# Small steps around the choice of the first expert's tokens, moved or shortened, and three index products put elsewhere

## The chip, the cores and the metric

The program runs on one core of a Trainium2 chip. The metric is the device time of one execution in microseconds (us); the time before is the median of three runs. The engines are PE (matrix products; PEld loads its weights), DVE (vector), ACT (scalar and activation), POOL (GpSimd) and SP, which here only issues DMAs. All engines run side by side, each takes its own instructions in order, and they meet through semaphores.

## What is computed

One layer of an encoder: a mixing sub-layer (half Fourier, half windowed attention), then a mixture of experts in which every expert picks its own tokens. The change touches the second sub-layer and the last tile of the first.

```python
D_MODEL, SEQ, N_EXPERTS, D_EXPERT, CAPACITY_FACTOR = 1024, 1024, 16, 1024, 2

def expert_choice_moe(h, w_router, w_gate, w_up, w_down):
    B, S, D = h.shape
    cap = CAPACITY_FACTOR * S // N_EXPERTS           # 128 tokens per expert
    aff = jax.nn.softmax(jnp.einsum('bsd,de->bse', h, w_router).astype(jnp.float32), axis=-1)
    g, idx = lax.top_k(aff.transpose(0, 2, 1), cap)
    xin = jax.vmap(lambda hb, ib: hb[ib])(h, idx)
    a = jnp.einsum('becd,edf->becf', xin, w_gate)
    u = jnp.einsum('becd,edf->becf', xin, w_up)
    y = jnp.einsum('becf,efd->becd', jax.nn.silu(a) * u, w_down)
    y = y * g[..., None].astype(y.dtype)
    return jax.vmap(lambda yb, ib: jnp.zeros((S, D), yb.dtype)
                    .at[ib.reshape(-1)].add(yb.reshape(-1, D)))(y, idx)

# in the layer:
x = x + g1 * mixed
h2 = rmsnorm(x, norm_ffn_g[l]) * (1.0 + sc2) + sh2
x = x + g2 * expert_choice_moe(h2, w_router[l], w_gate[l], w_up[l], w_down[l])
```

All arrays are float32.

## The kernel before

The 1024 tokens are eight tiles of 128. The mixing sub-layer goes over the tiles; `oproj(t)` is the output projection of a tile, after which `x2` (the residual stream) and `h2` (its normed and modulated copy) of the tile are known. `last_tile` does this for tile 7 in smaller steps: `x2` is flipped on PE and multiplied by the router's weights (L822, L832), POOL raises the mean square to the power -0.5 (`rs`, L837), and `affinity` makes the softmax `aff` of the tile (L883 to L893). The rest of `last_tile` makes `h2`: a product with `G2_r` on DVE (L838), a scaling by `rs` on ACT in two halves (L842, L850), an addition of `sh2_r` on POOL in two halves (L852), and then SP writes `h2` to the DRAM tensor `h2d` (L1271). Between these stand four 32-wide transposes that turn the ranked scores of the older tiles, `R`, into `bestw` (L844, L847).

`choose(e)` then finds, for one expert, the position that each token gets among its 128 chosen (`pos`), by counting on PE and DVE. It is called for expert 0 and, after expert 0's tokens are fetched, for expert 1. `gather_a(e)` (L1306) compares `pos` with the numbers 1 to 128 (`slots`) and makes a one-hot matrix `oneh`, eight compares of a 128x128 tile, on DVE for experts 0 to 3 and on POOL for the others. `gather(e)` multiplies the eight tiles of `oneh` with the token numbers and gates on PE (L1313, the index products), adds two columns to the index (L1317), and POOL fetches the 128 rows of `h2d` by an indirect DMA into the only buffer `xe` (L1319). `busy` issues bf16 products of no use that keep PE running (L1168).

Then come the experts. An expert is 12 products of 2 k-blocks each: four for `w_gate` (`ga`), four for `w_up` (`up`), four for `w_down`, the last four of expert e during expert e+1 (`put`). They are counted by `step[0]`: P0 to P3 are `ga` of expert 0, P4 to P7 its `up`, P8 to P11 `ga` of expert 1, P12 to P15 `put(0)`, P16 to P19 `up` of expert 1, P20 to P23 `ga` of expert 2, and so on. P0 to P5 are done in plain float32 from the loaded weights (L1292). The others use a split: ACT copies a unit of weights to a float32r part `wh` (L86), DVE subtracts to get the rest `wl` (L87), and PE does three products (L81 to L83). A split for a later product is issued as far ahead as four buffers of `wh` and `wl` allow. The gathered rows `xe` and the hidden values `hs` are flipped by `flip` (L1339, eight transposes into two PSUM banks named `pt`, of which there are only two in all) and split in the same way into `t0h`, `t0l`, `t1h`, `t1l`.

What belongs to the choice for experts 1 to 3 is the generator `selection`. `product` draws a number of steps from it ahead of each product (`rest`), so a `yield` in it is a place between two products. `thresholds` sorts the last two tiles' scores and finds the positions for the other 15 experts: a 16-wide diagonal `dg`, a product with it (L1259), the compares `gq` and the counting (L1174, L1176).

The order of the work is fixed at the end of the kernel: PE, DVE and POOL keep the written order from `mark[0]` (the start of `last_tile`) on, SP from the write of `h2d` on, ACT from `selection` on; before that a scheduler may place ACT's work. `tc.issue_after(i)` queues what is written in its block behind instruction `i` where both are on one engine; it makes no engine wait for another.

## Time and profile before

| | us |
|---|---|
| median of 3 runs | 981.7 (980.85 to 984.77) |
| the profiled execution | 983.92 |
| its span, first to last instruction | 982.1 |
| PE busy / DVE busy / ACT busy / POOL busy | 937.9 / 787.6 / 629.2 / 411.5 |

The profile's times are from the span's start. A row of the timeline gives start, duration, engine, line, operation, what it writes and reads, and in brackets how long the engine sat idle before it and whose event ended that. Several instructions of one kind in a row are one line (x8), whose duration runs from the first start to the last end. Plain float32 products stand as two instructions each. PEclk is the TensorE clock that was granted, 1.00 for 2.4 GHz and 0.50 for 1.2 GHz.

### The profile page before, as it was taken

How to read it: one execution, taken by the hardware profiler on the slowest of the kernel's cores; microseconds unless marked ns; L12 is line 12 of the kernel's file. 1: busy time of each engine (PE TensorE's matmuls, PEld its weight loads, DVE VectorE, ACT ScalarE, POOL GpSimd, SP SyncE). 2: the span in 40 equal slices, each digit the busy share in tenths (PEclk: the TensorE clock that was granted, in tenths of full speed). 3: DMA queues.
4: the chain of work that ended last, by engine and by line, in shares of the span. 5: the costliest groups of instructions: out<-in, count | busy, mean ns of one | idle time of the engine just before them, and what ended most of it. 6: DMA issues, size and time to landing. Idle time of an engine off the chain costs nothing.

```text
span 982.1 us, 13289 instructions
## 1 busy us (share of the span) xinstructions
PE 937.9 (95%) x4788; PEld 736.2 (75%) x4788; DVE 787.6 (80%) x1231; ACT 629.2 (64%) x839; POOL 411.5 (42%) x247
## 2 busy tenths in 40 slices
PE   4999999989999999899899999999999999999996
PEld 2678777657777776468788888888888888888885
DVE  1436787788777968988888988998898898889894
ACT  2464533657566653247578777777777777877771
POOL 1007455100000002203449767876976876792201
PEclk9999999989999999999999999999999999999998
DMA  8977556462222248699999999999999999999912
GB/s 283 345 259 269 183 207 223 135 191 81 80 76 93 76 177 317 255 408 408 357 358 409 383 387 404 393 385 385 411 387 388 408 384 388 389 407 384 386 65 44
DMA packets 91787, 283.98 MB, mean 289 GB/s; under 512 B 8156, under 2 KB 25744, under 8 KB 91592
## 3 DMA queue, kind: packets, MB, share of 16 engines
q1 hardware_dynamic: 86856, 266.32, 70.9%
q0 software_dynamic: 4864, 16.80, 6.7%
q8 instruction: 38, 0.62, 0.3%
q14 instruction: 29, 0.24, 0.1%
HBM read 263.79 MB, written 21.40 MB: 290 GB/s over the span
## 4 chain that ended last, share of the span: by engine, by line
PE 82%; DVE 9%; ACT 3%; DMA 2%; issue 1%; SPq 1%; POOLq 0%; POOL 0%; ACTq 0%; DVEq 0%
PE pa L81 17%; PE pa L83 17%; PE pa L82 17%; PE pu L376 6%; PE pt L1339 3%; PE pj L81 2%; PE yp L728 2%; PE pj L82 2%; PE pj L83 2%; DVE ws L123 2%; PE pt L715 2%; PE pa L1292 2%; PE lg L686 1%; DMA raw<-in_w_ada_dram 1%; PE pv L376 1%
## 5 line engine op out<-in xcount | busy, mean ns | idle before, releaser
L87 DVE TENSOR_TENSOR wl<-raw,wh 128x2048 fp32r<-128x2048 f32 (+1 forms) x189 | 422.6, 2267 | 53.9 <-ACT wh L86 52.9
L86 ACT ACTIVATE wh<-raw 128x2048 fp32r<-128x2048 f32 (+1 forms) x189 | 355.4, 1896 | 79.5 <-PE pa L82 62.6
L1306 POOL TENSOR_SCALAR oneh<-tri_f,pos 128x128 bf16<-128x128 f32 x96 | 212.5, 2228 | 15.1 <-PE pt L1313 14.7
L81 PE MATMUL pa<-wh,t1h 128*128 128x512 f32 x384 | 151.4, 394 | 0.0
L83 PE MATMUL pa<-wl,t1h 128*128 128x512 f32 x384 | 149.6, 390 | 0.0
L82 PE MATMUL pa<-wh,t1l 128*128 128x512 f32 x384 | 149.5, 389 | 0.0
L81 PE MATMUL pa<-wh,t0h 128*128 128x512 f32 x360 | 143.2, 398 | 0.0
L82 PE MATMUL pa<-wh,t0l 128*128 128x512 f32 x360 | 140.9, 391 | 0.0
L83 PE MATMUL pa<-wl,t0h 128*128 128x512 f32 x360 | 140.9, 391 | 0.0
L83 PEld LDWEIGHTS pa<-wl,t1h 128*128 128x128 f32 x384 | 72.1, 188 | 15.1
L82 PEld LDWEIGHTS pa<-wh,t1l 128*128 128x128 f32 x384 | 72.1, 188 | 14.3
L81 PEld LDWEIGHTS pa<-wh,t1h 128*128 128x128 f32 x384 | 72.1, 188 | 14.3
L83 PEld LDWEIGHTS pa<-wl,t0h 128*128 128x128 f32 x360 | 68.0, 189 | 14.3
L82 PEld LDWEIGHTS pa<-wh,t0l 128*128 128x128 f32 x360 | 68.0, 189 | 13.7 <-issue 0.2
L81 PEld LDWEIGHTS pa<-wh,t0h 128*128 128x128 f32 x360 | 68.0, 189 | 13.7 <-issue 0.2
L1319 POOL DMA_INDIRECT xe<-h2d,idx x16 | 18.4, 1147 | 136.4 <-DVE gt L1329 122.6
L809 POOL TENSOR_TENSOR rs<-ss,mhalf 128x1 f32<-128x1 f32 x7 | 3.9, 558 | 170.8 <-DVE ss L807 146.8
L1357 POOL DMA_INDIRECT out_dram<-ys,idx x15 | 49.3, 3287 | 45.9 <-DVE ys L1356 41.8
L1354 POOL TENSOR_TENSOR ys<-ys,g_r 128x512 f32<-128x512 f32 x28 | 50.0, 1804 | 43.1 <-ACT ys L1353 43.1
L278 ACT ACTIVATE hf<-pt,sh1c,G1c 128x128 f32<-128x128 f32 (+1 forms) x56 | 22.6, 482 | 35.6 <-PE pt L271 35.6
L376 PE MATMUL pu<-wh,hh 128*128 128x512 f32 x128 | 42.6, 417 | 1.0 <-ACT hh L86 0.9
L689 DVE CUSTOM_DVE_ANT_0 sb<-lg,bias,sink 128x384 f32<-128x384 f32 (+1 forms) x64 | 35.2, 579 | 9.9 <-PE lg L687 4.9
(344 smaller groups left out, 1644.2 us busy)
## 6 DMA issues: line engine op xcount, KB each, us to landing
raw<-in_w_gate_dram SPq DMA_DIRECT2D x64, 1024.0 KB, 9.1
raw<-in_w_up_dram SPq DMA_DIRECT2D x64, 1024.0 KB, 8.9
raw<-in_w_down_dram SPq DMA_DIRECT2D x63, 1024.0 KB, 8.8
raw<-in_w_ada_dram SPq DMA_DIRECT2D x16, 1024.0 KB, 7.6
raw<-in_w_ada_dram SPq DMA_DIRECT2D x16, 512.0 KB, 9.6
xt<-in_x_dram SPq DMA_DIRECT2D x8, 512.0 KB
raw<-in_w_out_dram SPq DMA_DIRECT2D x4, 1024.0 KB, 4.9
raw<-in_x_dram SPq DMA_DIRECT2D x8, 512.0 KB
```

What stands on the lines that cost most here:

```text
L81: PE.matmul(o, lh, rh, start=start, stop=False)
L82: PE.matmul(o, ll, rh, start=False, stop=False)
L83: return PE.matmul(o, lh, rl, start=False, stop=stop)
L86: ACT.activation(hi, src, AF.Copy)
L87: return (eng or DVE).tensor_tensor(lo, src, hi.bitcast(F32), op=OP.subtract)
L278: ACT.activation(hf[:, a * w:a * w + w], tp[:, a * w:a * w + w], AF.Identity, scale=G1c[:, kc:kc + 1], bias=sh1c[:, kc:kc + 1])
L376: PE.matmul(acc[:, :c1 - c0], lhs, r[kc][:, c0:c1], start=first, stop=(kc == 7 and r is w_l), skip_group_check=c0 == 1024)
L689: DVE.tensor_tensor_reduce(sb[:, :wid], lg[:, :wid], bias[:, kv * 4 + i, j0:j0 + wid], 1.0, sk[:, i:i + 1], op0=OP.add, op1=OP.max, accum_ ...
L1306: (POOL if t < shared else DVE).tensor_scalar(oneh[:, t, :], slots, pos[:, t, e:e + 1], None, op0=OP.is_equal)
L1339: PE.transpose(p[:, k * 128:k * 128 + 128], src[:, (4 * b + k) * 128:(4 * b + k + 1) * 128], ident)
L1354: POOL.tensor_tensor(ys[:, cs_], ys[:, cs_], g2_r[:, cs_], op=OP.mult)
L1357: POOL.indirect_dma_start(out=out2, out_offset=bass.IndirectOffsetOnAxis(ap=idx[:, :1], axis=0), in_=ys, in_offset=None, compute_op=OP.add)
```

## The change

In `last_tile`, PE gets two filling products of 128 columns ahead of the first pair of flips and one ahead of the second; the product with `G2_r` moves from ahead of `affinity` into `aside`, which stands between the maximum and the exponential; the four transposes of `R` all stand behind `affinity`; the copy `bestT` stands ahead of it; and POOL's two additions of `sh2_r` are written in a block `issue_after(after["aff"].ins)`. The numbers 1 to 128 are copied to bf16 (`slots_b`), and `gather_a` compares with that copy. In the experts, `xf` (the flipped rows of expert 0) is made in three parts, and the third, with the gate product of expert 0, moves behind P0; `selection` is drawn 0 steps ahead of P0, 1 ahead of P1, 5 up to P9 and 3 from then on; the index products of expert 1 move from behind P0 to behind P1, those of expert 2 from behind P12 to behind P11, and those of expert 3 from behind P21 to behind P15.

The order of DVE around the softmax of tile 7 before (`ss` is the mean square, `lg` the router's logits, `raw<-raw,G_r` the product with `G2_r`, `best` is `bestw`, `acc` the first count of `choose(0)`):

```order
L835 TENSOR_TENSOR ss<-ss 128x1
L838 TENSOR_TENSOR raw<-raw,G_r 128x512
L883 SCALAR_TENSOR_TENSOR lg<-pj,rs,cb 128x16
L885 TENSOR_REDUCE mx<-lg 128x1
L844 STREAM_TRANSPOSE best<-R 32x32 x3
L892 RECIPROCAL rsm<-sm 128x1
L893 TENSOR_SCALAR aff<-ex,rsm 128x16
L847 STREAM_TRANSPOSE best<-R 32x32
```

And now:

```order
L837 TENSOR_TENSOR ss<-ss 128x1
L885 SCALAR_TENSOR_TENSOR lg<-pj,rs,cb 128x16
L887 TENSOR_REDUCE mx<-lg 128x1
L844 TENSOR_TENSOR raw<-raw,G_r 128x512
L894 RECIPROCAL rsm<-sm 128x1
L895 TENSOR_SCALAR aff<-ex,rsm 128x16
L849 STREAM_TRANSPOSE best<-R 32x32 x4
```

The product with `G2_r` has changed places with three of the transposes. POOL's rows at this place are the same before and now, and the second addition waits for ACT alone in both; these are the rows now, with the semaphores that each waits for in brackets (DMAHW are DMA queues):

```order
L839 TENSOR_TENSOR rs<-ss,mhalf 128x1 [waits DVE_49,Pool_49]
L846 COPY bestT<-R 16x128
L854 TENSOR_TENSOR raw<-raw,sh_r 128x512 [waits DMAHW1_49,DMAHW0_49,DMAHW3_49,PE_49,Activation_49]
L854 TENSOR_TENSOR raw<-raw,sh_r 128x512 [waits Activation_49]
L1323 DMA xe<-h2d,idx 128x1024 [waits DMAHW3_49,DMAHW2_49,DMAHW4_49,DMASW0_49,DVE_49]
```

Neither addition waits for DVE, where `aff` is made. On ACT, whose order is not fixed here, the first half of the split of P6's weights now stands between the exponential and the second scaling of `h2`.

PE from the fetched rows of expert 0 to the index products of expert 1 before (`ys` is the storage of `xf`; L1384 is the gate product of expert 0, each of its eight and of the eight of L1313 with a weight load ahead):

```order
L1377 MATMUL pt<-ident,xe 128x128 x8
L1384 LDWEIGHTS oneh
L1384 MATMUL pt<-aux,oneh 128x4
...
L1292 MATMUL pa<-raw,ys 128x512 x4
L1313 LDWEIGHTS oneh
L1313 MATMUL pt<-aux,oneh 128x6
...
L937 MATMUL pt<-ident,aff 32x128
```

And now:

```order
L1382 MATMUL pt<-ident,xe 128x128 x4
L1296 MATMUL pa<-raw,ys 128x512 x4
L1382 MATMUL pt<-ident,xe 128x128 x4
L1394 LDWEIGHTS oneh
L1394 MATMUL pt<-aux,oneh 128x4
...
L1296 MATMUL pa<-raw,ys 128x512 x4
L1317 LDWEIGHTS oneh
L1317 MATMUL pt<-aux,oneh 128x6
```

Four plain products (P0) now stand ahead of the last four flips, and four more (P1) ahead of the index products of expert 1.

DVE from the diagonal `dg` to the one-hot matrix of expert 3 before (`cn` and `pos` come from the counting; `wl` is a split of one unit of weights):

```order
L1256 TENSOR_SCALAR dg<-ident,R 16x16
...
L1306 TENSOR_SCALAR oneh<-tri_f,pos 128x128 x8
L87 TENSOR_TENSOR wl<-raw,wh 128x2048 x3
...
L87 TENSOR_TENSOR wl<-raw,wh 128x2048 x6
L87 TENSOR_TENSOR t0l<-pt,t0h 128x512 x2
L87 TENSOR_TENSOR wl<-raw,wh 128x2048
L1424 TENSOR_TENSOR hs<-hs,pa 128x512 x2
L1306 TENSOR_SCALAR oneh<-tri_f,pos 128x128 x8
L87 TENSOR_TENSOR wl<-raw,wh 128x2048 x2
L87 TENSOR_TENSOR t1l<-pt,t1h 128x512 x2
```

And now:

```order
L1260 TENSOR_SCALAR dg<-ident,R 16x16
...
L87 TENSOR_TENSOR t0l<-pt,t0h 128x512 x2
L87 TENSOR_TENSOR wl<-raw,wh 128x2048
L1183 SCALAR_TENSOR_TENSOR cn_4683<-pa,gq_4611 128x240
L1268 TENSOR_TENSOR pos<-cn_4683 128x8x15
L1310 TENSOR_SCALAR oneh<-slots_b,pos 128x128 x8
L87 TENSOR_TENSOR wl<-raw,wh 128x2048
...
L87 TENSOR_TENSOR wl<-raw,wh 128x2048 x3
L1310 TENSOR_SCALAR oneh<-slots_b,pos 128x128 x8
```

The one-hot matrix of expert 3 has moved from behind the product `hs` of expert 1 (ahead of the two splits and the flip's rest `t1l`) to a place four splits behind that of expert 2; ahead of the latter stands one split more.

The diff:

```diff
--- before.py
+++ after.py
@@ -825,6 +825,8 @@
             DVE.tensor_tensor(h2[:, c], o[:, 256 * q:256 * q + 256], g1_r[:, c], op=OP.mult)
             DVE.tensor_tensor(x2[:, c], x2[:, c], h2[:, c], op=OP.add)
             f = pt()
+            for _ in range(2 - q):
+                PE.matmul(f[:, 256:384], ident, ident, start=True, stop=True)
             for k in range(2):
                 PE.transpose(f[:, k * 128:k * 128 + 128], x2[:, c.start + k * 128:c.start + k * 128 + 128], ident)
             ACT.activation(x2T[:, 4 + 2 * q:6 + 2 * q].rearrange("p a b -> p (a b)"), f[:, :256], AF.Copy)
@@ -835,21 +837,21 @@
         after["ss"] = DVE.tensor_tensor(ss[:, 0:1], ss[:, 0:1], ss[:, 1:2], op=OP.add)
         rs = p3.tile([128, 1], F32, name="rs", bufs=2)
         POOL.tensor_tensor(rs, ss[:, 0:1], mhalf[:, 0:1], op=OP.pow)
-        DVE.tensor_tensor(h2[:, 512:], x2[:, 512:], G2_r[:, 512:], op=OP.mult)
         R, = ranked
 
         def aside():
             ACT.activation(h2[:, :512], h2[:, :512], AF.Copy, scale=rs)
-            for b in range(3):
-                DVE.transpose(bestw[32 * b:32 * b + 32, :], R[:, 32 * b:32 * b + 32])
-
+            DVE.tensor_tensor(h2[:, 512:], x2[:, 512:], G2_r[:, 512:], op=OP.mult)
+
+        POOL.tensor_copy(bestT, R[:16])
         affinity(t, p, rs, aside)
-        DVE.transpose(bestw[96:, :], R[:, 96:])
-        POOL.tensor_copy(bestT, R[:16])
+        for b in range(4):
+            DVE.transpose(bestw[32 * b:32 * b + 32, :], R[:, 32 * b:32 * b + 32])
         with tc.issue_after(after["exp"].ins):
             ACT.activation(h2[:, 512:], h2[:, 512:], AF.Copy, scale=rs)
-        for c in (slice(0, 512), slice(512, D)):
-            POOL.tensor_tensor(h2[:, c], h2[:, c], sh2_r[:, c], op=OP.add)
+        with tc.issue_after(after["aff"].ins):
+            for c in (slice(0, 512), slice(512, D)):
+                POOL.tensor_tensor(h2[:, c], h2[:, c], sh2_r[:, c], op=OP.add)
         lastx.append((rows, x2, h2))
 
     def x2_flip(t, b, x2):
@@ -1135,7 +1137,9 @@
     aside = [POOL.tensor_copy(tri, r1_f)]
     tri_f = rt.tile([128, 3, 128], F32, name="tri_f")
     SP.dma_start(tri_f, t_in["k_tri"][1:4].rearrange("a p c -> p a c"))
-    slots, both = tri_f[:, 0, :], tri_f[:, 1:3, :].rearrange("p a c -> p (a c)")
+    slots_b = rt.tile([128, 128], BF, name="slots_b")
+    aside.append(POOL.tensor_copy(slots_b, tri_f[:, 0, :]))
+    both = tri_f[:, 1:3, :].rearrange("p a c -> p (a c)")
     below = tri_f[:, 2, :]
     ones_b = rt.tile([128, 128], BF, name="ones_b")
     aside.append(POOL.memset(ones_b, 1.0))
@@ -1283,7 +1287,7 @@
     def product(acc, xh, xl, la=3, halves=False):
         n = step[0]
         u = n % 4
-        drain(itertools.islice(rest, 5 if n < 9 else 3))
+        drain(itertools.islice(rest, 0 if n == 0 else 1 if n == 1 else 5 if n < 10 else 3))
         ahead(min(la, 1 + n // 2))
         step[0] += 1
         if n in PLAIN:
@@ -1303,7 +1307,7 @@
         shared = 0 if e < 4 else NT
         oneh = wk.tile([128, NT, 128], BF, name="oneh", bufs=1)
         for t in range(NT):
-            (POOL if t < shared else DVE).tensor_scalar(oneh[:, t, :], slots, pos[:, t, e:e + 1], None, op0=OP.is_equal)
+            (POOL if t < shared else DVE).tensor_scalar(oneh[:, t, :], slots_b, pos[:, t, e:e + 1], None, op0=OP.is_equal)
         return oneh
 
     def gather(e, oneh):
@@ -1371,30 +1375,35 @@
         cut_unit(2)
         cut_unit(2)
     xf = wk.tile([128, D], F32, name="ys", bufs=1).rearrange("p (k c) -> p k c", c=128)
-    for k0, n in ((0, 2), (2, 2), (4, 4)):
+
+    def xf_flip(k0, n):
         p = pt()
         for k in range(n):
             PE.transpose(p[:, k * 128:k * 128 + 128], gs[0][2][:, (k0 + k) * 128:(k0 + k + 1) * 128], ident)
         ACT.activation(xf[:, k0:k0 + n], p[:, :n * 128].rearrange("p (a b) -> p a b", b=128), AF.Copy)
+
+    xf_flip(0, 2)
+    xf_flip(2, 2)
     xh, xl = (wk.tile([128, 8, 128], F32R, name=f"t0{x}", bufs=1) for x in "hl")
 
+
     def selection():
+        xf_flip(4, 4)
         p = pt()
         for t in range(NT):
             PE.matmul(p[:, :4], oneh0[:, t, :], aux[:, t, 0, 2:], start=(t == 0), stop=(t == NT - 1))
         gates(0, p[:, :4])
-        yield from wait(4)
         split(xh, xl, xf)
         oneh = gather_a(1)
-        yield from wait(3)
+        yield
         gather(1, oneh)
         for _ in thresholds():
             yield
         for e in (2, 3):
-            while step[0] < 12 * e - 16:
+            while step[0] < 7 * e - 6:
                 yield
             o = gather_a(e)
-            yield from wait(7)
+            yield from wait(9 - 2 * e)
             gather(e, o)
 
     rest = selection()
```

## Rows read from the trace of the kernel before

**Rows 1.** The page's first part, busy time of each engine over the span.

```profile
PE 937.9 (95%) x4788; PEld 736.2 (75%) x4788; DVE 787.6 (80%) x1231; ACT 629.2 (64%) x839; POOL 411.5 (42%) x247
```

**Rows 2.** What PE waited for from 380 us to the end: who, for whom, us in total, times, longest.

```profile
PE pt L1313 <- DVE t1l L87: 3.6, 1, 3.6
PE pt L1313 <- DVE oneh L1306: 1.3, 2, 1.0
```

**Rows 3.** One stretch of the expert loop: its length, PE's busy time and instructions, granted clock, busy share of the DMA engines, GB/s.

```profile
540.00:575.00 35.00, 35.00 (x171) 1.00 1.03 390
```

**Rows 4.** Timeline around the softmax of tile 7.

```profile
387.76 0.68 DVE L838 TENSOR_TENSOR raw<-raw,G_r 128x512 f32<-128x512 f32 x1
387.99 0.87 POOL L837 TENSOR_TENSOR rs<-ss,mhalf 128x1 f32<-128x1 f32 x1 [2.15 <-DVE ss L835]
...
388.90 0.72 ACT L842 ACTIVATE raw<-raw,rs 128x512 f32<-128x512 f32 x1 [1.01 <-POOL rs L837]
...
389.26 0.62 DVE L844 STREAM_TRANSPOSE best<-R 32x32 f32<-32x32 f32 x3
...
389.70 2.50 POOL L852 TENSOR_TENSOR raw<-raw,sh_r 128x512 f32<-128x512 f32 x2 [0.60 <-ACT raw L842]
...
390.14 0.86 DVE L893 TENSOR_SCALAR aff<-ex,rsm 128x16 f32<-128x16 f32 x1
...
391.90 0.48 DVE L1205 SCALAR_TENSOR_TENSOR junk<-pt,best,ones 128x256 bf16<-128x256 f32 x1 [0.66 <-PE pt L1195]
```

**Rows 5.** The same two kinds of instruction in all tiles: shortest, median and longest in ns, first and last start in us.

```profile
L809 POOL TENSOR_TENSOR rs<-ss,mhalf x7: 548/548/599, 245.2 to 374.4; 128x1 f32<-128x1 f32 x7
...
L893 DVE TENSOR_SCALAR aff<-ex,rsm x8: 217/232/861, 253.1 to 390.1; 128x16 f32<-128x16 f32 x8
```

**Rows 6.** PE in single microseconds around the same place, columns as in the group of the expert loop.

```profile
385.00:386.00 1.00, 0.35 (x4) 1.00 1.02 410
...
389.00:390.00 1.00, 1.00 (x5) 0.50 1.03 410
```

**Rows 7.** Compares and scalings on DVE: total and mean of one (us, ns) for two widths of one scaling, and the eight compares of expert 0 in the timeline.

```profile
L704 DVE TENSOR_SCALAR sb<-sb,rin 128x384 f32<-128x384 f32 x48 | 16.9, 416 | 0.2
...
L704 DVE TENSOR_SCALAR sb<-sb,rin 128x256 f32<-128x256 f32 x16 | 4.6, 349 | 0.1
...
395.60 1.65 DVE L1306 TENSOR_SCALAR oneh<-tri_f,pos 128x128 bf16<-128x128 f32 x8
```

**Rows 8.** Timeline from the rows of expert 0 to the end of the plain products, and one stretch of it with the columns of the group of the expert loop.

```profile
402.10 4.71 DVE L87 TENSOR_TENSOR wl<-raw,wh 128x1024 fp32r<-128x1024 f32 x4
...
402.88 0.66 ACT L1378 ACTIVATE ys<-pt 128x256 f32<-128x256 f32 x2 [8.57 <-PE pt L1377]
...
404.64 1.06 ACT L86 ACTIVATE t0h<-ys 128x1024 fp32r<-128x1024 f32 x1
...
407.19 1.22 DVE L87 TENSOR_TENSOR t0l<-ys,t0h 128x1024 fp32r<-128x1024 f32 x1
...
408.67 1.55 PE L1313 MATMUL pt<-aux,oneh 128*128 128x6 bf16 x8 [0.98 <-DVE oneh L1306]
...
410.19 17.33 PE L1292 MATMUL pa<-raw,ys 128*128 128x512 f32 x40
410.26 0.22 DVE L1317 TENSOR_SCALAR idx<-pt 128x1 int32<-128x1 f32 x1 [0.28 <-PE pt L1313]
...
408.00:410.00 2.00, 1.22 (x7) 1.00 1.01 418
```

**Rows 9.** DVE from the sort of the last tiles to the splits behind the one-hot matrix of expert 2 (timeline), and from the chain of work that ended last (start, us) PE's flip of `hs` of expert 0 and the counting.

```profile
423.12 2.29 DVE L87 TENSOR_TENSOR wl<-raw,wh 128x2048 fp32r<-128x2048 f32 x1 [0.72 <-ACT wh L86]
...
431.37 1.29 DVE L87 TENSOR_TENSOR t1l<-pt,t1h 128x512 fp32r<-128x512 f32 x2 [1.87 <-ACT t1h L86]
...
432.95 0.22 DVE L1256 TENSOR_SCALAR dg<-ident,R 16x16 f32<-16x16 f32 x1
...
445.38 6.68 DVE L87 TENSOR_TENSOR wl<-raw,wh 128x2048 fp32r<-128x2048 f32 x3
...
439.91 0.87 PE pt L1339 x8
440.88 0.88 PE pa L1176 x15
```

**Rows 10.** Timeline around the index products of expert 3, and a stretch behind them with the columns of the group of the expert loop.

```profile
479.45 1.29 DVE L87 TENSOR_TENSOR t1l<-pt,t1h 128x512 fp32r<-128x512 f32 x2
...
475.58 1.04 PE L1339 MATMUL pt<-ident,hs 128*128 128x128 f32 x8
480.19 0.34 PE L1313 MATMUL pt<-aux,oneh 128*128 128x6 bf16 x8 [3.57 <-DVE t1l L87]
480.39 0.64 PE L81 MATMUL pa<-wh,t0h 128*128 128x512 f32 x1
...
484.11 0.39 PE L81 MATMUL pa<-wh,t0h 128*128 128x512 f32 x1
484.34 0.39 PE L82 MATMUL pa<-wh,t0l 128*128 128x512 f32 x1
...
482.00:484.00 2.00, 2.00 (x6) 0.51 1.04 414
```

**Rows 11.** POOL's compares from 490 to 925 us: busy time, mean ns of one, idle time ahead of them.

```profile
L1306 POOL TENSOR_SCALAR oneh<-tri_f,pos 128x128 bf16<-128x128 f32 x88 | 203.7, 2328 | 0.4
```

## Prediction

> **What bounds the kernel now.** The first part of the profile's page comes first: PE is busy for 937.9 of 982.1 us [rows 1]. The list of what PE waited for shows where it is not: from 380 us to the end there are two waits of size, both ahead of index products, 3.6 us once for a flip's rest on DVE and 1.0 us for a one-hot matrix [rows 2]. The expert loop has none: 35.00 of 35.00 us busy at full clock [rows 3]. So a microsecond that the choice of the first experts costs PE is a microsecond at the end, and the loop behind passes any gain on. Three places count: the chain from the softmax of tile 7 to the fetch of expert 0 (385 to 402 us), where PE only fills time; the start of the plain products (402 to 427.5); and the index products of experts 2 and 3 (427 to 484).
>
> **The softmax of tile 7.** The power on POOL took 0.87 us, in other tiles 0.55 [rows 4, 5]: it ended 0.42 after the product with `G2_r` (387.76 to 388.44), which ran on DVE beside it. With that product gone from there `rs` comes 0.32 earlier, and with it the logits, ACT's scaling and the exponential; the logits need PE's products too, done at about the same time. `aff` took 0.86 us where 0.23 is its median [rows 4, 5], and it ended (391.00) as POOL's first addition did (389.70 and half of 2.50, 390.95). So the two hold each other up. The change means to put the addition behind `aff`, but POOL's rows of the order show no wait for DVE. The addition still starts when ACT's scaling is done, now 388.58 + 0.72 = 389.3. There it meets the moved product with `G2_r` (0.68, from about 389.0 to 389.7), which by the power's example holds POOL up; the addition then runs from 389.7 to 390.9, `aff` wants to start at 389.87 and again ends at 390.95. Gain so far 0.05. Then come four transposes of 0.21 [rows 4], until 391.8, against the first count at 391.90. I take a gain of 0.1 us. The bounds: 1.0 if the addition does not hold `aff` up (390.1 + 0.83 = 390.9), and a loss of 0.3 if the count's next step is held by the second addition, which comes later because ACT now does a half split (about 1 us) ahead of its second scaling. That later addition delays the write of `h2d` by some 0.5 us, covered by the 5 us between the addition's end (392.2 [rows 4]) and the last compare of expert 0 (397.25 [rows 7]), behind which the fetch comes.
>
> The Trainium skill's page "SBUF — State Buffer" (section "SBUF: two separate sides") says that DVE and GpSimd share one pair of ports as an exclusive lock, for the whole of an instruction with two SBUF inputs. The two rows agree, 0.87 against 0.55 and 0.86 against 0.23. By the rule the moved product delays the addition and the front gains 0.1; without it the addition would end at 390.6, `aff` at 390.7, and the front would gain 0.4.
>
> The filling products: three of 128 columns, at most 0.8 us, lie in PE's idle time ahead of the flips (0.35 us busy from 385 to 386 [rows 6]) and cost nothing. After this lull the granted clock fell to 0.50 [rows 6]. If the fill keeps it at 1.00, PE's second flip of `aff` is done 0.5 us earlier, but DVE's four transposes end no sooner than 391.8, so I count nothing.
>
> **bf16 token numbers.** The eight compares stand on the chain, 1.65 us for eight, 0.2 apart [rows 7]. No row has a bf16 source. Of one instruction the part that depends on the width is 0.067 us for 128 elements (416 minus 349 ns [rows 7]), so the gain lies between 0 and 8 x 0.067 = 0.53; I take the middle, 0.3. The Trainium skill ("VectorE: DVE Perf Modes", section "The perf-mode tier table") gives `tensor_scalar` twice the speed on bf16 that it has on fp32 in SBUF; by that the gain is half of the width's part, an estimate of 0.27, the same term. The cast to `slots_b` lies in POOL's idle time before.
>
> **Plain products and index products of expert 1.** On the trace's own axis: before, the index products waited 0.98 us and then took 1.55 at the compares' pace [rows 8], where eight such products with the weights at hand take 0.34 [rows 10]. Now P0 starts once ACT's first copy is done, 403.3 (it was 404.0). Forty plain instructions take 17.33 us [rows 8], so a product of eight takes 3.45: P0 ends at 406.7, the last flips and the gate product (0.45 + 0.34) at 407.5, P1 at 410.95. DVE ends its four half splits at 406.8 and now waits for ACT: third copy 407.8, `t0h` (1.06) 408.9, `t0l` (1.2) 410.1, compares 411.45. The index products end at 411.55, a flip of `aff` takes 0.1, and P2 to P5 (13.75) end at 425.4; before, they ended at 427.5. Gain 2.1. It would be 1.2 if the compares stayed the last to come by another microsecond, and 2.6 if nothing waited.
>
> **Index products of expert 2.** DVE is now later and PE earlier. The index of expert 1 comes at 411.65 instead of 410.26; from there to `dg` DVE had 22.9 us with 2.6 of waiting [rows 8, 9], so 20.3 of work: `dg` is done at 432.0, and PE comes for it behind P8, at 434.5 (425.4, three products of twelve at 0.23 [rows 10], 2.75 each, a flip of 0.87 [rows 9]). Then DVE does three splits more, 2.22 each (6.68 for three [rows 9]), `hs` and `t0l` (1.2 each), `gq` 0.4, one more split than before ahead of the compares, the counting's 0.75 and the compares 1.4: 13.85, so 432.0 becomes 445.85. PE, one product earlier than before, is there at 445.05 (425.4, six products, two flips, about 1.4 for the product with `dg` and the counting, 0.88 of it in [rows 9]). It waits 0.8 us. Nothing between zero (DVE 4% faster) and one split, 2.2, is excluded.
>
> **Index products of expert 3.** Before, they stood behind the flip of `hs`, whose two banks were free only when DVE, late with two splits, had done the flip's rest: 3.57 us of wait [rows 10]. After it the clock was 0.51 [rows 10]: nine products from 480.39 to 484.11, 3.72 us where nine at 0.23 take 2.07, a loss of 1.65. Now they stand behind P15. DVE needs 10.9 us from 445.85 (four splits, the index, the compares), done at 456.7; PE is there at 446.1 + 11.0 = 457.1. No wait. Behind the flip of `hs` now comes a product that needs nothing from it; the banks are wanted next ten products later. Gain 5.2. On POOL the fetch for expert 3 then waits until `xe` is flipped behind P18, about 8 us, with expert 4's compares behind it; these need 8 x 2.33 = 19 us [rows 11] and are wanted at P31, some 38 us after that flip.
>
> **Sum**: -0.1 - 0.3 - 2.1 + 0.8 - 5.2 = -6.9 us. The profiled execution took 983.92, so 977.0 of its kind; it lies 2.2 above the median of 981.7, for which I forecast 974.8. The loads of weights start again when expert 0's rows land, 0.4 us earlier, and lie at a DMA share of 1.03 in the loop [rows 3], but PE never waits for one from 380 us on [rows 2].
>
> **Rivals.** (a) DVE's room is smaller than my sums: the index products of expert 2 wait one split longer, 2.2, and the clock falls behind that wait as it did after 3.57 us, 1.7: -6.9 + 3.9 = -3.0, 978.7. For it speaks that my sums leave DVE no idle time from 411.65 to 456.7; against it, that the wait of 0.98 us at 408 brought no lower clock [rows 8]. (b) The addition misses `aff` after all: 1.0 instead of 0.1, 973.9; the issue order speaks against it. (c) The weights, at a share of 1.03, are the true bound and take the gain back: 981.4; against it that PE has no wait for weights. (d) Slower: POOL's compares of experts 4 to 15 read bf16 too. If POOL takes longer on it, PE waits for each one-hot matrix. POOL does 19 us of compares per 35 us and about 8 of other work; from 3.3 us for one compare on (2.33 now) it is late, and at 4 us it loses 0.7 x 8 = 5.6 us for each of 11 experts, 62 in all: 1037. Against it: the change of source type removes bytes.
>
> **Chances.** Forecast 0.55 (its own range 973.0 to 976.8), (a) 0.23, (b) 0.12, (c) 0.05, (d) 0.05. Half a per cent is 4.9 us, about what a measurement of this kernel can tell from no change: below 976.8 is faster. That takes the forecast but for 0.04, (b) and 0.03 of (a): 0.66; the same gets 0.29, slower 0.05. The range of 8 in 10 reaches from (b) with a little more to (a) with a little more: 972.8 to 979.7.
>
> **What would show it.** In the profile after: `aff` still near 0.86 us beside POOL's addition; compares 0.16 apart; P5's end some 2.5 us earlier; a wait of about 1 us ahead of the index products of expert 2, none at those of expert 3; granted clock 1.00 from 470 to 490. I am wrong if the wait of 3.6 us only changes its place, if the clock falls behind the new wait, or if POOL's compares grow.

## The result, and the profile after

The changed kernel takes 976.78 us (median of 6 runs, 975.15 to 978.33), the kernel before 982.18 beside it (6 runs): a ratio of 0.9938, 95% interval 0.9926 to 0.9951, or 5.4 us faster (4.8 to 7.3). The forecast was 974.8 in a range of 972.8 to 979.7. The profiled execution took 977.43 (span 975.5), 6.5 less than that of before; the forecast's sum for it was 6.9.

The work ahead of tile 7 is the same in all kernels here but for one cast on POOL, yet their profiled executions start tile 7's last work up to 4 us apart (two executions of one kernel up to 2.6), so the stages are read from one mark to the next. The marks are four: the first work on tile 7 (product `raw<-lg,g_r` on line 825), the landing of expert 0's rows (PE's flip of `xe`), the flip of expert 1's rows, and the second flip of `hs`. The timeline of before at the two marks that the rows ahead of the prediction lack, and between them the logits:

```profile
385.20 0.41 DVE L825 TENSOR_TENSOR raw<-lg,g_r 128x256 f32<-128x256 f32 x1
...
388.90 0.23 DVE L883 SCALAR_TENSOR_TENSOR lg<-pj,rs,cb 128x16 f32<-128x16 f32 x1 [0.46 <-POOL rs L837]
...
402.43 0.63 PE L1377 MATMUL pt<-ident,xe 128*128 128x128 f32 x4 [0.64 <-DMA xe<-h2d,idx]
```

The timeline of the changed kernel at the steps that the prediction speaks of:

```profile
385.55 0.41 DVE L825 TENSOR_TENSOR raw<-lg,g_r 128x256 f32<-128x256 f32 x1
...
388.29 0.57 POOL L839 TENSOR_TENSOR rs<-ss,mhalf 128x1 f32<-128x1 f32 x1 [2.32 <-DVE ss L837]
...
388.90 0.23 DVE L885 SCALAR_TENSOR_TENSOR lg<-pj,rs,cb 128x16 f32<-128x16 f32 x1 [0.77 <-POOL rs L839]
...
389.69 1.37 POOL L854 TENSOR_TENSOR raw<-raw,sh_r 128x512 f32<-128x512 f32 x1 [0.60 <-ACT raw L843]
...
390.14 0.96 DVE L895 TENSOR_SCALAR aff<-ex,rsm 128x16 f32<-128x16 f32 x1
...
391.96 0.48 DVE L1209 SCALAR_TENSOR_TENSOR junk<-pt,best,ones 128x256 bf16<-128x256 f32 x1
...
395.66 1.38 DVE L1310 TENSOR_SCALAR oneh<-slots_b,pos 128x128 bf16<-128x128 bf16 x8
...
395.97 0.18 PE L1317 MATMUL pt<-aux,oneh 128*128 128x2 bf16 x1 [0.31 <-DVE oneh L1310]
...
402.32 0.63 PE L1382 MATMUL pt<-ident,xe 128*128 128x128 f32 x4 [0.74 <-DMA xe<-h2d,idx]
...
403.21 3.70 PE L1296 MATMUL pa<-raw,ys 128*128 128x512 f32 x8 [0.26 <-ACT ys L1383]
...
410.90 0.96 PE L1317 MATMUL pt<-aux,oneh 128*128 128x6 bf16 x8
...
428.34 1.03 PE L1343 MATMUL pt<-ident,xe 128*128 128x128 f32 x8
...
437.96 1.34 PE L1343 MATMUL pt<-ident,hs 128*128 128x128 f32 x8
...
474.81 1.03 PE L1343 MATMUL pt<-ident,hs 128*128 128x128 f32 x8
```

The power takes 0.57 (0.87 in [rows 4]); `aff` still takes 0.96 and ends with POOL's first addition (391.10 and 391.06); the eight compares take 1.38 instead of 1.65 [rows 7]. The index products of expert 1 take 0.96 and follow P1 without a wait, where they waited 0.98 and took 1.55 [rows 8].

What PE waited for in the changed kernel from 380 us to the end (us in total, times, longest):

```profile
PE pa L1218 <- DVE kept L1213: 1.1, 2, 0.7
PE pt L1199 <- DVE aff L895: 0.9, 1, 0.9
...
PE pt L1317 <- DVE oneh L1310: 0.3, 1, 0.3
```

The 0.3 in the last line is the first index product of expert 0 (at 395.97 above). One stretch around the second flip of `hs` there: its length, PE's busy time and instructions, granted clock, busy share of the DMA engines, GB/s.

```profile
470.00:490.00 20.00, 20.00 (x94) 1.00 1.03 393
```

The wait of 3.6 us ahead of expert 3's index products [rows 2] is gone, PE is busy without a gap there, and the clock of 0.51 behind it [rows 10] with it.

Stage by stage (before, after, difference): first work on tile 7 to the landing 17.23, 16.77, -0.46; landing to the flip of expert 1's rows (430.11 before) 27.68, 26.02, -1.66; from there to the second flip of `hs` (475.58 before [rows 10]) 45.47, 46.47, +1.00; from there to the end of the span 506.5, 500.7, -5.83. Expert 3's index products (0.35) passed from the fourth stage to the third; like for like these are +0.65 and -5.5. The sum is -6.95; with a start 0.35 later this is the 6.6 between the spans. In the first stage the first count comes 0.29 earlier, the compares save 0.27, and the fetch takes 0.10 longer.

### The profile page after: what moved, and what is told of

It is laid out like the page before. It is cut to its first block, busy times and chain, and to the rows that moved or that the text cites. A ratio compares the mean times of both kernels' runs of the same rounds, so it can differ in the third digit from the quotient of the medians.

```text
span 975.5 us, 13301 instructions
## 1 busy us (share of the span) xinstructions
PE 935.5 (96%) x4792; PEld 735.6 (75%) x4794; DVE 788.2 (81%) x1231; ACT 629.6 (65%) x839; POOL 416.9 (43%) x248
## 4 chain that ended last, share of the span: by engine, by line
PE 82%; DVE 8%; DMA 4%; ACT 3%; issue 1%; SPq 1%; POOLq 0%; POOL 0%; ACTq 0%; DVEq 0%
PE pa L81 17%; PE pa L83 17%; PE pa L82 17%; PE pu L376 5%; PE pt L1343 3%; DVE ws L123 2%; PE pj L81 2%; PE pj L82 2%; PE pj L83 2%; PE yp L728 2%; PE pa L1296 2%; PE pt L715 2%; PE lg L686 1%; DMA raw<-in_w_ada_dram 1%; PE lg L687 1%
## 5 line engine op out<-in xcount | busy, mean ns | idle before, releaser
L1310 POOL TENSOR_SCALAR oneh<-slots_b,pos 128x128 bf16<-128x128 bf16 x96 | 217.9, 2283 | 0.5
```

Source lines behind the costliest of these rows:

```text
L1310: (POOL if t < shared else DVE).tensor_scalar(oneh[:, t, :], slots_b, pos[:, t, e:e + 1], None, op0=OP.is_equal)
```

## Experiment 1: the index products of expert 3, back, alone, and with the stall filled

Three runs. `exp3_back` undoes this step alone in the changed kernel:

```diff
-            while step[0] < 7 * e - 6:
+            while step[0] < 12 * e - 16:
...
-            yield from wait(9 - 2 * e)
+            yield from wait(5 if e == 2 else 7)
```

> The changed kernel with the index products of expert 3 alone put back behind the flip of hs. Theory (the forecast's largest term, 5.2): the wait of about 3.6 us for DVE's rest of that flip is back, and behind it the granted clock is near 0.5 for about 4 us (another 1.65); the time is 5.2 above the changed kernel's 976.8, 982.0, a ratio to the kernel before of 0.9995. Rival 1, the wait comes back but the clock stays at 1.00: +3.6, ratio 0.998. Rival 2, DVE has caught up by then through the other parts: the wait is under 0.5 us, ratio 0.994, and the gain of the whole change comes from its other parts.

Measured: 981.28 us, ratio 0.9982 (0.9969 to 0.9995): 4.3 us lost by time instead of the 5.2 expected. Its twelve executions spread from 977.88 to 983.19. `b_exp3` makes this step alone in the kernel before (threshold `7 * e - 6`, a wait of 3 for expert 3):

> The kernel before with the move of expert 3's index products alone. Theory: this one move carries most of the gain; the wait of 3.6 us and the low clock behind it go, PE's time from the flip of hs to the end falls from 506.5 us to about 501, time -5.2 to -5.5, ratio 0.9945. Rival 1: DVE, which in this kernel has its old order up to here, is late at the new place as well, a wait of 1 to 2 us appears there or at the next flip, ratio 0.996. Rival 2: the other parts are needed for it, ratio 0.999.

Measured: 978.52 us, ratio 0.9952 (0.9939 to 0.9966), 4.7 us faster. `exp3_fill` is `exp3_back` with PE kept busy in the stall; the filling products go into the sum that the next real product starts anew (the lines that hand this sum on are left out here):

```diff
             yield from wait(5 if e == 2 else 7)
+            if e == 3:
+                early.append([pa(), pa()])
+                for _ in range(14):
+                    PE.matmul(early[0][0], ones_b, hot, start=True, stop=True)
             gather(e, o)
```

> The changed kernel with expert 3's index products put back behind the flip of hs, as in the earlier run, and with 14 filling products of 512 bf16 columns (0.22 us each, 3.1 us, into a sum that the next real product starts anew) in PE's stall ahead of them. It tells the stall's two costs apart. Theory: the lower clock follows from PE's idleness; with the stall filled the granted clock stays at 1.00, the nine to fourteen slow products behind it go, and of the 6.0 us that the old place cost in the earlier run (3.3 wait, 2.7 clock) only 3.3 stay: from the flip of hs to the end 504 to 505 us, ratio 0.9972. Rival: the clock falls all the same, as it did in the front in spite of filling products; 507 us, ratio 0.998 or more.

Measured: 979.07 us, ratio 0.9960 (0.9946 to 0.9974), 2.2 us faster than `exp3_back` by the ratios, whose intervals still touch. PE's timeline at that place in `exp3_back`:

```profile
471.67 1.04 PE L1343 MATMUL pt<-ident,hs 128*128 128x128 f32 x8
476.00 0.35 PE L1317 MATMUL pt<-aux,oneh 128*128 128x6 bf16 x8 [3.29 <-DVE t1l L87]
```

The same in `exp3_fill` (the trace has 13 of the 14 filling products):

```profile
472.47 1.04 PE L1343 MATMUL pt<-ident,hs 128*128 128x128 f32 x8
473.56 2.97 PE L1410 MATMUL pa<-hot,ones_b 128*128 128x512 bf16 x13
476.81 0.34 PE L1317 MATMUL pt<-aux,oneh 128*128 128x6 bf16 x8 [0.28 <-DVE t1l L87]
```

Windows of PE (columns as above) in `exp3_back`, then in `exp3_fill`, then in `b_exp3`:

```profile
470.00:490.00 20.00, 16.71 (x74) 0.83 0.99 386
476.00:482.00 6.00, 6.00 (x22) 0.50 1.02 408
```

```profile
470.00:490.00 20.00, 19.67 (x98) 1.00 1.02 412
```

```profile
470.00:490.00 20.00, 20.00 (x94) 1.00 1.03 388
```

From the flip of `hs` to the end it takes 507.5 us in `exp3_back` (span 979.2), 504.6 in `exp3_fill` (977.1), 501.0 in `b_exp3` (976.5) and 500.7 in the changed kernel. So the stall costs 3.3 and the low clock behind it 2.9, and the second falls away when PE has something to do in the stall, though that work computes nothing. `b_exp3` shows that the step needs none of the other parts, and that no wait takes its place: its rivals fall, but for 0.23 us that the index products of expert 3 take more there (0.58) than in the changed kernel. By time the step is worth 4.7 us out of the 5.4; by the trace 5.5 out of 6.95. The old place cost more clock in `exp3_back` (6.8 us at 0.50, summed from single microseconds) than in before (3.4), so this term differs between executions. At half the clock, 3.4 us lose 1.7.

## Experiment 2: the start of the plain products put back

`plain_back` flips all of expert 0's rows ahead of the first plain product again and gives the selection its old pace:

```diff
-        drain(itertools.islice(rest, 0 if n == 0 else 1 if n == 1 else 5 if n < 10 else 3))
+        drain(itertools.islice(rest, 5 if n < 9 else 3))
     xf_flip(2, 2)
+    xf_flip(4, 4)
...
-        xf_flip(4, 4)
...
+        yield from wait(4)
         split(xh, xl, xf)
         oneh = gather_a(1)
-        yield
+        yield from wait(3)
```

> The changed kernel with the start of the plain products alone as before (all three flips of expert 0's rows ahead of the first plain product, index products of expert 1 at the old place, old pace of DVE's and PE's side work). Theory (forecast: -2.1 at expert 1, +0.8 at expert 2): the index products of expert 1 wait about 1 us and run at the compares' pace (about 1.55 us), the first plain product starts 0.8 us later; the wait at expert 2's index products goes. Time +1.3, 978.1, ratio 0.9951. Rival 1, the wait at expert 2 was nothing and stays nothing: +2.1, ratio 0.996. Rival 2, what PE gains at the start it loses again behind it to DVE: +0, ratio 0.9938.

Measured: 975.87 us, ratio 0.9937 (0.9924 to 0.9950): by time no loss at all, where the theory gave 1.3 us; this is what rival 2 expected. PE's timeline:

```profile
399.15 0.63 PE L1382 MATMUL pt<-ident,xe 128*128 128x128 f32 x4 [0.65 <-DMA xe<-h2d,idx]
...
405.18 1.32 PE L1317 MATMUL pt<-aux,oneh 128*128 128x6 bf16 x8 [0.76 <-DVE oneh L1310]
...
426.39 1.04 PE L1343 MATMUL pt<-ident,xe 128*128 128x128 f32 x8
436.02 1.03 PE L1343 MATMUL pt<-ident,hs 128*128 128x128 f32 x8
443.44 0.35 PE L1317 MATMUL pt<-aux,oneh 128*128 128x6 bf16 x8
...
472.18 1.04 PE L1343 MATMUL pt<-ident,hs 128*128 128x128 f32 x8
```

From the landing to the flip of expert 1's rows it takes 27.24, so the new placing gains 1.22 there (26.02). To the second flip of `hs` it is 73.03 against 72.49 (after): 0.54 is left. What went in between stands in the rows: the flip of `hs` of expert 0 takes 1.34 in the changed kernel and 1.03 here, and the index products of expert 2 take 0.70 in the changed kernel (at 445.73) and 0.35 here. PE, earlier, meets DVE twice. This is the wait forecast at expert 2, in two places and 0.66 in all instead of 0.8. The time can't tell 0.54 from nothing, so in the trace the step is worth less than half of what the theory gave it, and by time nothing is shown.

## Experiment 3: token numbers in fp32

```diff
-    slots_b = rt.tile([128, 128], BF, name="slots_b")
-    aside.append(POOL.tensor_copy(slots_b, tri_f[:, 0, :]))
+    slots_b = tri_f[:, 0, :]
```

> The changed kernel with the token numbers in fp32 again (no cast, compares read fp32). Theory (forecast -0.3): the eight compares of expert 0 take 1.65 instead of 1.38 us, the index and the landing of expert 0's rows come 0.27 later; time +0.3, ratio 0.9941, at the edge of what five rounds tell. Rival: PE's part of the chain (a weight load and a product for each compare, with a filling product between) sets the pace and not DVE: the index comes at the same time, +0. POOL's compares of experts 4 to 15 mean about 2.3 us in both theories.

Measured: 976.69 us, ratio 0.9943 (0.9930 to 0.9956), not to be told from the changed kernel. In the trace the eight compares of each of the experts 0 to 3 take 0.26 or 0.27 more. DVE's row for expert 0, and PE's index products of experts 1 to 3:

```profile
393.15 1.65 DVE L1309 TENSOR_SCALAR oneh<-tri_f,pos 128x128 bf16<-128x128 f32 x8
...
408.67 1.23 PE L1316 MATMUL pt<-aux,oneh 128*128 128x6 bf16 x8
...
443.76 0.96 PE L1316 MATMUL pt<-aux,oneh 128*128 128x6 bf16 x8
...
455.60 0.58 PE L1316 MATMUL pt<-aux,oneh 128*128 128x6 bf16 x8
```

The index of expert 0 comes 1.92 us after the start of its compares, against 1.66 in the changed kernel, so DVE sets the pace and the rival falls. From the landing (400.12) to the second flip of `hs` (473.38) it takes 73.26, 0.77 more than in the changed kernel: the index products of experts 1 to 3 take 0.27, 0.26 and 0.23 longer, at the pace of the compares. With expert 0's the bf16 numbers are worth about 1.0 us on the trace's axis and not 0.3; the time doesn't show it.

## Experiment 4: the fill, the additions, and the clock of the front

`no_fill` (run twice) drops the three filling products in `last_tile`. `after_again` is the changed kernel once more. `add_idx2` (run twice) adds two steps to the changed kernel, `more_fill` (run twice) a third:

```diff
+        tiny = p3.tile([128, 1], F32, name="tiny", bufs=1)
         with tc.issue_after(after["aff"].ins):
+            POOL.tensor_copy(tiny, aff[:, t, 0:1])
             for c in (slice(0, 512), slice(512, D)):
...
-            yield from wait(9 - 2 * e)
+            yield from wait(8 if e == 2 else 3)
```

```diff
-                busy(4)
-        busy(2)
+                busy(5)
+        busy(2 if e else 5)
```

> The changed kernel without the three filling products ahead of the last flips of tile 7. Theory (forecast: counted nothing): the granted clock falls to 0.50 between 389 and 391 us as it did before, PE's products there take twice as long, but DVE's first count still starts when its four transposes end, near 391.9; time within 0.3 us of the changed kernel, ratio 0.9938. Rival: the clock at 1.00 is what kept the front early; without it the second flip of aff comes 0.5 us later and the count with it, ratio 0.9943 and the first count near 392.4.

> The changed kernel once more, on the chip of the three runs above, for its ratio beside theirs and for a second look at the granted clock in the lull of tile 7. Ratio 0.9938 as before. If the filling products decide the clock there, it stays at 1.00 as in the first profile; if not (in three profiles of variants with the same fill it fell to 0.50 for 3 to 8 us, without the fill for 3 and for 11 us) it falls here too, and the way from the first work on tile 7 to the landing of expert 0's rows grows from 16.8 to as much as 17.6 us.

> The changed kernel with two steps more: POOL reads one column of aff (a copy of 128 values) ahead of its two additions, so that they really start behind aff, and the index products of expert 2 stand one product later. Theory: the addition is what held aff up (0.96 us), so aff takes about 0.25, the four transposes and the first count come 0.7 us earlier, and from the first work on tile 7 to the landing of expert 0's rows it takes 16.1 us instead of 16.8; the index products of expert 2 take 0.35 instead of 0.70 us and wait for nothing. Time -1.0 against the changed kernel, ratio 0.9928. Rival 1: the additions now hold up the transposes or the first count instead, the front gains nothing: -0.35. Rival 2: the later additions make the write of h2d and the fetch late: slower by up to 1 us, ratio 0.995.

> The run add_idx2 with four filling products of 512 bf16 columns more (0.22 us each at full clock) in PE's idle time of the front: one ahead of the second flip of aff (0.94 us idle there in the changed kernel's second profile), three ahead of the first product with kept (0.69 idle). Theory: the granted clock of the front follows PE's idleness, as behind the stall of expert 3, where the fill held it at 1.00; with less idle time it stays at 1.00, aff's early end is passed on, and from the first work on tile 7 to the landing of expert 0's rows it takes 16.1 us (16.8 to 17.3 in the changed kernel's two profiles): time -0.7 to -1.2 against the run add_idx2, ratio 0.992. Rival 1: the clock falls to 0.50 all the same, the fill then takes twice its time and stands in the chain: 17.0 to 17.6 us, ratio 0.9926 to 0.993. Rival 2: the clock stays but the fill delays the flip of aff or the product with kept by up to 0.4: 16.5 us.

> The run add_idx2 once more, beside the run with more fill. Theory: aff takes 0.23 us and the index products of expert 2 0.35 us again; where the clock falls in the front differs from execution to execution, so the way from the first work on tile 7 to the landing of expert 0's rows lies anywhere between 16.1 (clock 1.00) and 17.3 us; ratio 0.9926 again. Rival: the fall at 386.7 us, about 3.2 us after the first work on tile 7, comes at the same place again, since it belongs to the kernel and not to the execution.

> The run more_fill once more. If the fill is what held the granted clock at 1.00 in the front, it stays at 1.00 here too, and from the first work on tile 7 to the landing of expert 0's rows it takes 16.1 us again. If the first profile was luck, as the changed kernel's first profile was (1.00 there, 0.50 for 7 us in its second), the clock falls and the way takes 16.4 to 17.3. Ratio 0.9927 again.

> The changed kernel without its three filling products once more. If the long fall of the clock in the first profile (0.50 from 384 to 395 us, 17.95 us from the first work on tile 7 to the landing of expert 0's rows) belongs to the missing fill, it comes again, 17.5 to 18 us, ratio 0.9945; if it belongs to the execution, 16.8 to 17.4 us as with the fill, ratio 0.9936.

Measured: `no_fill` 0.9936 (0.9924 to 0.9949) and 0.9926 (0.9912 to 0.9941); `after_again` 0.9933 (0.9920 to 0.9947); `add_idx2` 0.9926 (0.9912 to 0.9939) and 0.9929 (0.9916 to 0.9943); `more_fill` 0.9927 (0.9914 to 0.9941) and 0.9922 (0.9907 to 0.9938). No two of these intervals are apart, so the rest is read from the traces. For each profile with the new front: PE's time at a granted clock of 0.50 between 380 and 400 us, summed from single microseconds, and the way from the first work on tile 7 to the landing.

| kernel | at 0.50, us | way, us |
|---|---|---|
| changed | none | 16.77 |
| `exp3_back` | 3.4 | 16.84 |
| `after_again` | 6.8 | 17.33 |
| `exp3_fill` | 6.8 | 17.52 |
| `plain_back` | 6.8 | 17.58 |
| `f32_slots` (its compares 0.27 longer) | 6.8, in two falls | 17.12 |
| `no_fill`, both | 10.2, 10.2 | 17.95, 18.04 |
| `add_idx2`, both | 3.4, 3.4 | 17.05, 16.39 |
| `more_fill`, both | none, none | 16.08, 16.08 |

Windows of PE (columns as above) of `after_again`, then of the two runs without fill, then of the second run with more of it:

```profile
391.00:397.00 6.00, 6.00 (x41) 0.50 0.34 136
```

```profile
384.00:394.00 10.00, 9.35 (x47) 0.50 0.69 275
```

```profile
388.00:397.00 9.00, 8.96 (x48) 0.50 0.60 239
```

```profile
386.00:397.00 11.00, 9.93 (x71) 1.00 0.79 315
```

The same code of the front ran once without a fall and four times with one, of 3 or 7 us, and a fifth time with fp32 compares; without the fill it fell twice for 10, and with four fills more it did not fall in two executions. The old front, which has no fill either, fell for 3.4 us in both its profiles (before and `b_exp3`, way 17.23 and 17.42), so the fill alone does not set the length of the fall. How the low clock gets into the chain is seen in three timelines. The second run without fill, then the first `add_idx2`:

```profile
387.96 0.23 DVE L883 SCALAR_TENSOR_TENSOR lg<-pj,rs,cb 128x16 f32<-128x16 f32 x1 [1.10 <-PE pj L832]
...
389.10 1.05 DVE L893 TENSOR_SCALAR aff<-ex,rsm 128x16 f32<-128x16 f32 x1
```

```profile
387.37 0.23 DVE L887 SCALAR_TENSOR_TENSOR lg<-pj,rs,cb 128x16 f32<-128x16 f32 x1 [1.10 <-PE pj L834]
...
388.51 0.23 DVE L897 TENSOR_SCALAR aff<-ex,rsm 128x16 f32<-128x16 f32 x1
388.66 0.84 DVE L849 STREAM_TRANSPOSE best<-R 32x32 f32<-32x32 f32 x4
388.88 0.19 POOL L854 COPY tiny<-aff 128x1 f32<-128x1 f32 x1 [1.65 <-DVE aff L897]
389.11 2.50 POOL L856 TENSOR_TENSOR raw<-raw,sh_r 128x512 f32<-128x512 f32 x2
390.03 0.48 DVE L1211 SCALAR_TENSOR_TENSOR junk<-pt,best,ones 128x256 bf16<-128x256 f32 x1 [0.53 <-PE pt L1201]
...
446.72 0.35 PE L1319 MATMUL pt<-aux,oneh 128*128 128x6 bf16 x8
```

And the index of expert 0 in `after_again`, where the clock fell only behind the first count:

```profile
395.26 0.22 DVE L1321 TENSOR_SCALAR idx<-pt 128x1 int32<-128x1 f32 x1 [0.65 <-PE pt L1317]
```

In the first two the logits wait 1.10 us and for PE, no longer for `rs` as in the kernels before and after; they come 0.55 us later after the first work on tile 7 than in the changed kernel. In `after_again` the first count comes as early as in the changed kernel, but its counting and index products at half clock bring the index 0.47 later. Late logits can also change who waits for whom: in the first run without fill POOL's addition started ahead of the moved product with `G2_r`, which then took 1.77 us instead of 0.68, and `aff`, now behind the addition, took 0.23:

```profile
385.59 1.26 POOL L852 TENSOR_TENSOR raw<-raw,sh_r 128x512 f32<-128x512 f32 x1 [0.60 <-ACT raw L841]
385.63 1.77 DVE L842 TENSOR_TENSOR raw<-raw,G_r 128x512 f32<-128x512 f32 x1
...
387.51 0.23 DVE L893 TENSOR_SCALAR aff<-ex,rsm 128x16 f32<-128x16 f32 x1
```

In `add_idx2` a real dependence puts the additions behind `aff`, and `aff` takes 0.23: the addition was what held it. The transposes and the count take their usual time beside the additions, so rival 1 falls; so does rival 2, since from the index to the landing it takes 5.13 and 5.08 us (5.00 and 5.09 in the two profiles of the changed kernel). But the logits are 0.55 late and the count now waits 0.53 for PE's flip, both at half clock, and the 0.7 won is lost there; in the second execution, where the fall came later, the way is 16.39. With more fill the clock stays up, the gain is passed on, and the way is 16.08 twice, as forecast for it (16.1). The second step works as expected: the index products of expert 2 take 0.35 and PE meets nothing there; from landing to the second flip of `hs` it takes 72.22 instead of 72.49.

The two ratios of `more_fill` each lie 0.0011 under one of the changed kernel's (0.9938 and 0.9933), 1.1 us. Its stages up to the second flip of `hs` are 1.0 to 1.6 us shorter in the traces, but by time it isn't shown to be faster, neither than the changed kernel nor than `add_idx2`, against which 0.7 to 1.2 us were expected. Nor does the time show the loss of `no_fill`, 0.6 to 1.3 us against the two profiles of the changed kernel: whether the clock falls as often in unprofiled runs stays open.

## Why the prediction was right, and where it wasn't

- *What bounds the kernel.* Right. PE's waits decided: the loop passed the gains on (from the second flip of `hs` to the end it takes 500.5 to 501.0 us in all eleven profiles with expert 3's new place, however early they reach that flip), its DMA share stayed at 1.03 with 6 us less span, and rival (c) is out. POOL's compares of experts 4 to 15 (88, between 490 and 925 us) mean 2.327 us as in [rows 11], so rival (d) is out.
- *Expert 3, -5.2.* Right in mechanism and size: -5.5 in the trace, -4.7 alone by time (interval 3.3 to 6.0), and `exp3_fill`, one profile, shows its two parts apart, wait and clock. PE came for the index products at 457.26, worked out was 457.1.
- *Expert 1, -2.1.* Oversized: -1.66. The first plain product (403.21, forecast 403.3) and the start of the index products (410.90, 410.95) came as worked out, but these end at 411.86 and not at 411.55, since DVE's compares begin and end later than worked out (at 411.63 instead of 411.45); P2 to P5 then take 13.90 and not 13.75 (32 of the 40 instructions in the 17.33 of [rows 8] are 13.86). Some 0.4 of the 1.66 is not of the placing: `plain_back` has it too, and about half of it is the bf16 compares (`f32_slots` loses 0.23 there). The sign given for P5, some 2.5 us earlier, came out as 2.1 counted from the first work on tile 7.
- *Expert 2, +0.8.* Right in size: 0.66, in two places (the flip of `hs` 0.31 longer, the index products 0.35). The place was half wrong: only the index products were named, and no wait stands ahead of them, they are longer at the pace of the compares. Rival (a), one split more and a clock fall, did not come.
- *The additions and `aff`, -0.1.* Right in mechanism, too small in size: they still collide, and `add_idx2` shows the addition to be the cause, but the first count comes 0.29 earlier, counted from the first work on tile 7. `rs` is 0.35 earlier (worked out 0.32), and the moved product held the addition up by 0.12 (1.37 instead of half of 2.50), where the sum had let it start only at the product's end, 0.4 later. The page "SBUF — State Buffer" of the Trainium skill (section "SBUF: two separate sides") says that DVE, in an operation that uses both ports or has two inputs in SBUF (these only against a GpSimd operation that reads SBUF), and GpSimd shut each other out for a whole instruction. The traces agree: `aff` takes 0.96 beside the addition and 0.23 without, and in the first run without fill the moved product, which came second there, takes 1.77 instead of 0.68.
- *bf16, -0.3.* Right: for expert 0 the compares take 0.27 less and the index comes 0.26 earlier. What `f32_slots` loses at experts 1 to 3 (0.77) is no missing term of the sum, because the sums for experts 1 and 2 already had the short compares (1.35 and 1.4); only the expectation for `f32_slots` left it out.
- *The fill, "I count nothing".* This step failed as far as the traces go. It stood on DVE's transposes as the last to come; at half clock PE's logits are late first, and the transposes with them. Without fill the way is 0.6 to 1.3 us longer than in the two profiles of the changed kernel; with two executions on either side, it is not shown that the fill is what makes the difference.
- *The total.* The profiled executions differ by 6.5 where 6.9 was worked out. That this is so close is in part luck: expert 1 gave 0.4 less than worked out, the additions and experts 2 and 3 together about 0.6 more. The medians differ by 5.4, and the forecast time lies 2.0 under the measured one; the interval of the ratio (4.8 to 7.3) holds 6.9. By time expert 3's step alone is worth 4.3 to 4.7 instead of the trace's 5.5. Executions also differ by some microseconds ahead of tile 7 and in the clock of the front, which is enough for the rest; it was not isolated.

## What to carry to other kernels

When PE waits a few microseconds for an engine that is late by a little, look for the same instruction's place a few products earlier or later before shortening anything: here moving eight small products was worth 4.7 us of the 5.4 by time. Price the stretch behind a stall too, since the low clock cost half as much as the stall in one profile (1.7 beside 3.6) and nearly as much in another (2.9 beside 3.3). And when PE is about to meet another engine several times in a row, what is gained at the first meeting is partly paid back at the next, so follow a gain to the loop before counting it.

## What the runs showed of the hardware

The granted clock of the same front code differed between executions, from no fall to 7 us at 0.50, with nothing changed in the work ahead of it, so a single profile does not show what an edit does to the clock. Behind expert 3's stall one execution with filling products showed no fall, and in the front both executions with the most of them; that it is the fill which holds the clock is likely from this, and more executions would be needed to show it for the front. Kernels with the same work ahead of tile 7 reached it between 381.4 and 385.6 us: spans of single profiles differ by more than most of the edits tried here, and only stages between marks can be compared.
